# Drawn orders of weight tiles and drawn places of moving tiles in a two-layer decoder trunk

## The chip, the cores and the metric

The kernel runs on one core of one Trainium2 chip. TensorE (PE) multiplies, VectorE (DVE), ScalarE (ACT) and GpSimd (POOL) do the elementwise work, and the queue of SyncE (SP) starts most DMAs. The metric is the device time of one execution in microseconds; lower is better. All arrays are laid out on the host before the launch, so the order in which weights lie in memory can be chosen freely.

## What is computed

The reference is a trunk of two layers over 256 tokens of width 2048, in float32. Layer 0 mixes tokens with a convolution module, layer 1 with causal stick-breaking attention of 16 heads; each is followed by a gated MLP with a depthwise convolution of width 3. Cut to what matters:

```python
for i in range(DEPTH):
    shift, scale, gate = ada_ln(c, mix_mod_w[i], mix_mod_b[i])
    h = rms_norm(x, mix_norm_g[i]) * (1.0 + scale) + shift
    if i % N_MIXERS == 0:
        y = conformer_conv_module(h, ...)    # h @ pw1, gate, conv of width 31, layer norm, silu, @ pw2
    else:
        y = stick_breaking_mixer(h, ...)     # h @ qkv, attention per head, @ o
    x = x + gate * y
    shift, scale, gate = ada_ln(c, ffn_mod_w[i], ffn_mod_b[i])
    h = rms_norm(x, ffn_norm_g[i]) * (1.0 + scale) + shift
    u = causal_depthwise_conv(h @ up_w[i], ...)
    gt, val = jnp.split(u, 2, axis=-1)
    x = x + gate * ((jax.nn.silu(gt) * val) @ down_w[i])
return rms_norm(x, final_norm_g)
```

Widths: the up product gives 2 x 5632 columns, the down product takes 5632 rows.

## The kernel before

**Tiles.** Activations are held transposed, as 128 features by 256 tokens. A product has an output for each 128 columns of its weight matrix (a block of outputs, `nb`) and sums over tiles of 128 rows (`kt`). A weight tile of 128 x 128 is the stationary operand, an activation tile the moving one. There are 16 tiles of the normed input `h` (and of `z`, the convolution module's second input), 44 of the gated MLP's `g`, worked on in two halves of 22, and 16 of the heads' results `o`.

**Split numbers.** Weights and activations are each split into a rounded part and a rest (`wh`, `wl`; `xh`, `xl`), held in a 4-byte type that TensorE multiplies in one pass. A unit of work, one weight tile with one activation tile, is wh·xh + wh·xl + wl·xh. In `gemm` (L270) this is done in one of two forms. As a triple it is three matmuls of 256 columns (L303, L304, L305). As a pair, where `both` is given, one matmul of 512 columns runs over xh and xl together, into a bank with room for both (L298), and one of 256 follows (L299). The second convolution product, the up products of layer 0, and the last output block of each down product run as triples; the down products, the later q and k products, the output projection and layer 1's up products run as pairs.

**Where the halves lie.** `halved` (L374) gives the tiles of z, g and o: one SBUF tile of 2 x HP floats, HP = 264, with the first half at 0 and the second at HP. `h_tiles` (L361) lays h out in the same way. So a tile takes 2112 bytes of each partition, and the next tile of a pool starts 2112 bytes further on. The g tiles stand in a ring of 23 (`g{j % NG}`); z and o have 16 tiles each.

**Order.** `plan` (L46) writes down, for each stage, the order of (output, tile). The first few outputs (`first`) are taken together, tile by tile, so that they can start before all inputs are ready, and they end one after the other on their last `stagger` tiles. The outputs behind them come one by one, each over its tiles in the order of their numbers. `Cfg` (L60) makes the plans: `pw1` and `pw2` for the convolution module, `up{i}0a` to `up{i}1b` and `down{i}0`, `down{i}1` for the MLP of layer i, `qk{g}a`, `qk{g}b` and `v{g}` for groups of four heads, and `o`.

**Streams.** Eight weight tiles make a piece of 512 KB. `_pack` lays the pieces out in the plan's order on the host, `load_next` (L227) loads them in order on SP's queue into a ring of six, `split_next` (L236) splits a piece on ScalarE (L243) and VectorE (L247), and `gemm` takes them piece by piece. When the last tile of an output is done, `done` moves the result on: `pw2_done`, `up_done` (which makes a g tile, L1011 to L1013), `down_done`, `qk_done`, `o_done`. Heads run beside the products, piece by piece (`attention`), and leave their results in o tiles (L1142 to L1145). Modulation vectors are computed on VectorE from streamed matrices (L337), paced by the pieces.

**Stages in time**, from the order of the matmuls, in us from the span's start: first convolution product and convolution to 285, `pw2` to 407, up and down products of layer 0 to 1152, q, k, v and attention to 1452, output projection to 1544, up and down products of layer 1 to 2286, end of the kernel at 2299.

Of the kernel before, what the change touches and what calls it, by code (L numbers as in the profile page):

```python
# [2 lines left out]

# [8 lines left out]
F32R = mybir.dt.float32r  # L12
# [4 lines left out]
P = 128  # L17
# [4 lines left out]
FIRST = 4  # L22
STAGGER = 2
# [19 lines left out]
MORE_MODS = 2  # L43


def plan(nbs, kts, first, stagger=4):  # L46

    seq = []
    if first > 1:
        head, nbs = nbs[:first], nbs[first:]  # L50
        s = min(stagger, len(kts) // 2)
        seq += [(n, k) for k in kts[:len(kts) - s] for n in head]
        seq += [(n, k) for n in head for k in kts[len(kts) - s:]]
    return seq + [(n, k) for n in nbs for k in kts]


class Cfg:
    def __init__(self, D, T, H, F, CW, FW):
        self.D, self.T, self.H, self.F, self.CW, self.FW = D, T, H, F, CW, FW
        KD = self.KD = D // P  # L60
        KF = self.KF = F // P
        self.GH = 4
        self.rows0 = min(ROWS, KD // 4)

        def columns(items):
            cols, n = {}, 0
            for name, k in items:
                cols[name] = (n, n + k)
                n += k
            return cols, n  # L70

        items = []
        items += [("mix_g1", KD), ("mix_b1", 3 * KD)]
        for i in range(2):
            items += [(f"ffn_g{i}", KD), (f"ffn_b{i}", 3 * KD)]
        for i in range(2):
            items += [(f"fdw{i}", 2 * KF * FW), (f"fdb{i}", 2 * KF)]
        items += [("fin_g", KD)]
        self.cols, self.ncols = columns(items)
        items = [("c", KD), ("mix_g0", KD), ("mix_b0", 3 * KD), ("pw1_b", 2 * KD), ("cdw", KD * CW), ("cdb", KD), ("ln_g", KD), ("ln_b", KD),  # L80
                 ("pw2_b", KD)]
        self.ccols, self.nccols = columns(items)

        kd = list(range(KD))
        pl = {}
        pairs = [n for j in range(KD) for n in (j, j + KD)]
        pl["pw1"] = plan(pairs, kd, min(HEAD, 2 * KD), 0)
        pl["pw2"] = plan(kd, kd, 8)
        self.halves = [list(range(KF // 2)), list(range(KF // 2, KF))]
        for i in range(2):  # L90
            for h, js in enumerate(self.halves):
                up = [n for j in js for n in (j, j + KF)]
                if h == 0:
                    pl[f"up{i}0a"] = plan(up[:FIRST], kd, FIRST, STAGGER)
                    pl[f"up{i}0b"] = plan(up[FIRST:], kd, 2, STAGGER)
                else:
                    pl[f"up{i}1a"] = plan(up[:2], kd, 1)
                    pl[f"up{i}1b"] = plan(up[2:], kd, 1)
                pl[f"down{i}{h}"] = plan(kd, js, 4)
        GH = self.GH  # L100
        for g in range(H // GH):
            hs = list(range(g * GH, (g + 1) * GH))
            qk = [n for h in hs for n in (h, H + h)]
            pl[f"qk{g}a"] = plan(qk[:FIRST], kd, FIRST if g == 0 else 1, STAGGER)
            pl[f"qk{g}b"] = plan(qk[FIRST:], kd, 1)
            pl[f"v{g}"] = [(2 * H + h, k) for k in kd for h in hs]
        pl["o"] = plan(kd, list(range(H)), 4)
        self.plans = pl
        order = ["pw1", "pw2", "up00a", "up00b", "up01a", "down00", "up01b", "down01"]
        for g in range(H // GH):  # L110
            order += [f"qk{g}a", f"v{g}"] if g == 0 else [f"v{g}", f"qk{g}a"]
            order.append(f"qk{g}b")
        self.order = order + ["o", "up10a", "up10b", "up11a", "down10", "up11b", "down11"]
# [3 lines left out]
def hybrid_trunk(ctx: ExitStack, tc: tile.TileContext, cfg: Cfg, io: dict):  # L117
    nc = tc.nc
    D, T, H = cfg.D, cfg.T, cfg.H
# [23 lines left out]
    def t256(name="t", bufs=6):  # L143
        return tmp.tile([P, T], F32, name=name, bufs=bufs)
# [23 lines left out]
    def pc(name, i0=0, n=None):  # L168
        if name in cfg.ccols:
            t, (a, b) = cpar["t"], cfg.ccols[name]  # L170
        else:
            t, (a, b) = par, cfg.cols[name]
        return t[:, a:b] if n is None else t[:, a + i0:a + i0 + n]
# [61 lines left out]
    def split_next(later=False):  # L235

        blocks, v, n = raws[len(parts)]
        if stream[len(parts)][0] == "pw1":
            parts.append((blocks, v, None))
            return  # L240
        wh = w_pool.tile([P, PW], F32R, name="wh")
        wl = w_pool.tile([P, PW], F32R, name="wl")
        nc.scalar.copy(wh[:, :n], v[:, :n])  # L243
        parts.append((blocks, wh, wl))

        def low():
            nc.vector.tensor_tensor(wl[:, :n], v[:, :n], wh[:, :n].bitcast(F32), op=ALU.subtract)  # L247

        if later:
            return low  # L250
        low()
# [111 lines left out]
    HP = T + 8  # L363
# [7 lines left out]
    def h_pairs():  # L371
        return [pairs[k] for k in range(KD)]

    def halved(pool, name):  # L374

        v = pool.tile([P, 2 * HP], F32R, name=name).rearrange("p (a t) -> p a t", a=2)[:, :, :T]
        return v[:, 0], v[:, 1], v

    def split_act(t, hh, hl, bias=None):

        if bias is None:
            nc.scalar.copy(hh, t)
            nc.vector.tensor_tensor(hl, t, hh.bitcast(F32), op=ALU.subtract)
        else:
            nc.scalar.activation(hh, t, AF.Identity, bias=bias)
            nc.vector.scalar_tensor_tensor(hl, t, bias, hh.bitcast(F32), op0=ALU.add, op1=ALU.subtract)
# [113 lines left out]
    with ExitStack() as cv:  # L500
# [141 lines left out]
        gb = cpool.tile([P, KD], F32, name="gb")  # L642
# [200 lines left out]
        for c in range(KD + 1):  # L843
# [6 lines left out]
            if c > 0:  # L850
                old = [(c - 1, k) for k in vector_taps(c - 1)[split(c - 1):]]
                n = max(len(taps), len(old))
# [3 lines left out]
            for s in range(nd):  # L856
# [10 lines left out]
                if c == 0 and s % 2 == 1 and 2 + s // 2 < NH:  # L867
                    j = 2 + s // 2
# [5 lines left out]
                if c == KD and s == 0:  # L874
                    low = split_next(later=True)
# [66 lines left out]
        zpool = cpar["z"] = cv.enter_context(tc.tile_pool(name="z", bufs=1))  # L942
        zs, zt = [], []
        for j in range(KD + 1):
            if j < KD:
                zt.append(t256())
                if j > 1:
                    nc.vector.tensor_tensor(ys[j], ys[j], dm, op=ALU.subtract)
                nc.vector.tensor_tensor(zt[j], ys[j], rs, op=ALU.mult)
                nc.scalar.activation(zt[j], zt[j], AF.Silu, bias=pc("ln_b", j, 1), scale=pc("ln_g", j, 1))  # L950
            if j == 1:
                low()
            if j > 0:
                zs.append(halved(zpool, f"z{j - 1}"))
                split_act(zt[j - 1], *zs[j - 1][:2])
            if j in (1, 2, 4):
                split_next()
# [18 lines left out]
    def ffn(i, entry, out):  # L976
        m = f"ffn{i}"
        NG = KF // 2 + 1
        LAST = (KD - 1,)
        with ExitStack() as fs:  # L980
            gpool = fs.enter_context(tc.tile_pool(name=f"g{i}", bufs=1))
            if i == 0:
                more["pool"] = fs.enter_context(tc.tile_pool(name="mods", bufs=MORE_MODS))
            gh, gl, gb = [None] * KF, [None] * KF, [None] * KF
# [17 lines left out]
            def up_done(nb, ps, both=False):  # L1002
                pend[nb] = conv3(ps, nb, both)
                j = nb % KF
                if not (j in pend and j + KF in pend):
                    return
                yg, yv = pend.pop(j), pend.pop(j + KF)
                s = t256()
                nc.scalar.activation(s, yg, AF.Silu)
                nc.vector.tensor_tensor(s, s, yv, op=ALU.mult)  # L1010
                gh[j], gl[j], gb[j] = halved(gpool, f"g{j % NG}")  # L1011
                nc.scalar.copy(gh[j], s)
                nc.vector.tensor_tensor(gl[j], s, gh[j].bitcast(F32), op=ALU.subtract)  # L1013

            def down_done(h):
# [15 lines left out]
                return done  # L1031

            hh, hl = entry.product(f"up{i}0a", up_done, "silu_and_others")
            both = h_pairs() if i else None
            rest = (lambda nb, ps: up_done(nb, ps, True)) if i else up_done
# [48 lines left out]
    with ExitStack() as at:  # L1084
        apool = at.enter_context(tc.tile_pool(name="attn", bufs=1))
# [3 lines left out]
        oh, ol, ob = [None] * H, [None] * H, [None] * H  # L1089
        CO = T + P  # L1090
        qk, vs = {}, {}
# [5 lines left out]
        def attention(h):  # L1097
            q, k, v, vc = qk[h], qk[H + h], vs[h // GH], (h % GH) * P
# [4 lines left out]
            z = zp[:, :CO]  # L1103
# [27 lines left out]
            a = t2.tile([P, CO], F32, name="e", bufs=3)  # L1131
# [7 lines left out]
            nc.tensor.matmul(op[:, 0:P], v[:, 0, vc:vc + P], a[:, 0:P], start=True, stop=True)  # L1139
            nc.tensor.matmul(op[:, P:T], v[:, 0, vc:vc + P], a[:, P:T], start=True, stop=False)  # L1140
            nc.tensor.matmul(op[:, P:T], v[:, 1, vc:vc + P], a[:, T:CO], start=False, stop=True)
            oh[h], ol[h], ob[h] = halved(apool, f"o{h}")  # L1142
            with tc.high_priority(offset=PRIORITY):
                nc.scalar.copy(oh[h], op[:, :T])
                nc.vector.tensor_tensor(ol[h], op[:, :T], oh[h].bitcast(F32), op=ALU.subtract)  # L1145
# [77 lines left out]
    for h in range(2):  # L1223
        t = slice(h * HT, (h + 1) * HT)
        nc.vector.reciprocal(rs[:, t], std[:, t])
        v = mpool.tile([P, D], F32, name="mraw")[:, :KD * HT].rearrange("p (k t) -> p k t", k=KD)
# [129 lines left out]
```

## Time and profile before

| What | Value |
|---|---|
| Median of 3 runs | 2299.14 us (2298.94 to 2299.4) |
| The profiled execution | 2300.79 us, its span 2299.1 us |
| VectorE, ScalarE, GpSimd busy | 1791.5, 1219.0, 409.9 us |
| Matmul and weight-load instructions | 14466 each |
| DMA | 603.16 MB, mean 262 GB/s |
| `up01b`, layer 0, 672 triples | 790.78 to 1025.98 us |
| `up11b`, layer 1, 672 pairs | 1927.78 to 2162.98 us |
| `down10`, layer 1, 330 pairs and 22 triples | 1804.52 to 1927.78 us |

The span runs from the first to the last instruction; the time of the execution is 1.7 us longer. A busy engine in the profile is one with an instruction under way. Matmuls overlap one another in the pipeline, so the mean duration of a matmul in a group is longer than the time from its start to the next one's start; how fast TensorE goes is read from the starts.

### The profile page before, as it was taken

The numbers are of one execution on the slowest core, as the hardware profiler recorded it, in microseconds if no ns is written. First come the engines' busy times: TensorE is split into PE (matmuls) and PEld (weight loads), VectorE is DVE, ScalarE is ACT, GpSimd is POOL, SyncE is SP. The second block draws the span as 40 slices with busy tenths as digits, with TensorE's granted clock in tenths as the row PEclk, the third lists the DMA queues.
The fourth block names the chain that finished last, engine by engine and source line by source line (L and its number), as shares of the span: only waits on it lengthen the run. The fifth ranks groups of instructions, "written<-read, shape, count | busy, mean of one in ns | idle before, by whom it ended". The sixth has DMA issues, their size and how long they took to land.

```text
span 2299.1 us, 37839 instructions
## 1 busy us (share of the span) xinstructions
PE 2265.5 (99%) x14466; PEld 2018.9 (88%) x14466; DVE 1791.5 (78%) x2504; ACT 1219.0 (53%) x1930; POOL 409.9 (18%) x534
## 2 busy tenths in 40 slices
PE   7999999999999999999999999999999999999997
PEld 5888678999998999998898888888888888888887
DVE  7689968989998899999975555779899655777654
ACT  2056655755544455554465555657555544555553
POOL 4058713200003100003411100112000010000031
PEclk9999999999999999999999999999999999999999
DMA  9988798789899989888865555566777665656663
GB/s 396 417 335 303 274 364 349 277 302 338 332 347 338 333 331 341 334 335 303 279 184 161 165 174 172 168 188 234 240 282 275 194 191 185 191 184 189 189 190 110
DMA packets 139144, 603.16 MB, mean 262 GB/s; under 512 B 15441, under 2 KB 15569, under 8 KB 115153
## 3 DMA queue, kind: packets, MB, share of 16 engines
q1 hardware_dynamic: 120242, 464.42, 57.8%
q0 software_dynamic: 18720, 136.32, 16.0%
q8 instruction: 113, 1.85, 0.3%
q14 instruction: 69, 0.57, 0.1%
HBM read 598.58 MB, written 2.10 MB: 261 GB/s over the span
## 4 chain that ended last, share of the span: by engine, by line
PE 86%; DVE 7%; DMA 4%; ACT 1%; issue 1%; POOL 0%; DVEq 0%; SPq 0%; ACTq 0%; POOLq 0%
PE ps L298 32%; PE ps L299 16%; PE ps L303 9%; PE ps L304 9%; PE ps L305 8%; PE ps L689 5%; DMA mraw<-in_mt_mix 3%; DVE mraw L337 3%; DVE wl L247 2%; PE ps L1181 1%; PE ps L1180 1%; PE ps L1179 1%; PE ps L581 1%; DMA raw<-in_w_pw 1%; DMA mraw<-in_mt_ffn 1%
## 5 line engine op out<-in xcount | busy, mean ns | idle before, releaser
L247 DVE TENSOR_TENSOR wl<-raw,wh 128x1024 fp32r<-128x1024 f32 x688 | 848.3, 1239 | 305.0 <-ACT wh L243 303.2
L243 ACT CAST wh<-raw 128x1024 fp32r<-128x1024 f32 x688 | 719.1, 1047 | 665.6 <-PE ps L298 290.2
L298 PE MATMUL ps<-h,wh 128*128 128x512 f32 x1760 | 619.0, 394 | 0.0
L299 PE MATMUL ps<-h,wl 128*128 128x256 f32 x1760 | 493.7, 281 | 0.0
L298 PE MATMUL ps<-g,wh 128*128 128x512 f32 x1320 | 462.5, 394 | 0.0
L303 PE MATMUL ps<-h,wh 128*128 128x256 f32 (+1 forms) x1504 | 421.7, 280 | 0.0
L304 PE MATMUL ps<-h,wh 128*128 128x256 f32 (+1 forms) x1504 | 420.5, 280 | 0.0
L305 PE MATMUL ps<-h,wl 128*128 128x256 f32 (+1 forms) x1504 | 419.0, 279 | 0.1
L298 PEld LDWEIGHTS ps<-h,wh 128*128 128x128 f32 x1760 | 330.5, 188 | 74.4
L337 DVE CUSTOM_DVE_ANT_0 mraw<-mraw,csr 128x2048 f32<-128x2048 f32 x152 | 349.9, 2302 | 30.9 <-DMA mraw<-in_mt_mix 28.7
L299 PE MATMUL ps<-g,wl 128*128 128x256 f32 x1320 | 370.7, 281 | 1.8 <-DVE wl L247 1.6
L299 PEld LDWEIGHTS ps<-h,wl 128*128 128x128 f32 x1760 | 332.3, 189 | 0.2
L298 PEld LDWEIGHTS ps<-g,wh 128*128 128x128 f32 x1320 | 247.8, 188 | 56.6
L304 PEld LDWEIGHTS ps<-h,wh 128*128 128x128 f32 x1504 | 284.7, 189 | 0.1
L305 PEld LDWEIGHTS ps<-h,wl 128*128 128x128 f32 x1504 | 282.5, 188 | 0.7 <-DVE wl L247 0.7
L303 PEld LDWEIGHTS ps<-h,wh 128*128 128x128 f32 x1504 | 282.4, 188 | 0.1
L299 PEld LDWEIGHTS ps<-g,wl 128*128 128x128 f32 x1320 | 249.3, 189 | 3.6 <-DVE wl L247 3.6
L689 PE MATMUL ps<-h,raw 128*128 128x256 f32 x832 | 188.8, 382 | 0.0
L689 PEld LDWEIGHTS ps<-h,raw 128*128 128x128 f32 x832 | 157.8, 191 | 28.3 <-issue 6.7
L1020 POOL TENSOR_TENSOR x<-x,t 128x256 f32<-128x256 f32 x56 | 69.3, 1237 | 533.8 <-ACT t L1019 533.7
L998 DVE SCALAR_TENSOR_TENSOR t<-t,par 128x254 f32<-128x254 f32 (+1 forms) x184 | 88.9, 483 | 46.6 <-ACT t L995 43.7
L729 DVE SCALAR_TENSOR_TENSOR auxb<-u,cpar,auxb 128x256 f32<-128x256 f32 x297 | 121.6, 483 | 4.5 <-ACT auxb L713 3.7
(272 smaller groups left out, 2741.6 us busy)
## 6 DMA issues: line engine op xcount, KB each, us to landing
raw<-in_w_down SPq DMA_DIRECT2D x176, 512.0 KB, 4.1
mraw<-in_mt_ffn POOLq DMA_DIRECT2D x64, 1024.0 KB, 6.4
raw<-in_w_pw SPq DMA_DIRECT2D x96, 512.0 KB, 7.9
mraw<-in_mt_mix POOLq DMA_DIRECT2D x48, 1024.0 KB, 7.8
raw<-in_w_up01b SPq DMA_DIRECT2D x84, 512.0 KB, 6.4
raw<-in_w_up11b SPq DMA_DIRECT2D x84, 512.0 KB, 3.6
raw<-in_w_up00b SPq DMA_DIRECT2D x80, 512.0 KB, 6.2
raw<-in_w_up10b SPq DMA_DIRECT2D x80, 512.0 KB, 4.6
```

The costliest lines, as they stand in the source:

```text
L243: nc.scalar.copy(wh[:, :n], v[:, :n])
L247: nc.vector.tensor_tensor(wl[:, :n], v[:, :n], wh[:, :n].bitcast(F32), op=ALU.subtract)
L298: nc.tensor.matmul(o, wh[:, c], both[kt], start=first, stop=False, skip_group_check=True)
L299: nc.tensor.matmul(o[:, :T], wl[:, c], xh[kt], start=False, stop=left[nb] == 0, skip_group_check=True)
L303: nc.tensor.matmul(o, wh[:, c], xh[kt], start=first, stop=False, skip_group_check=halves > 0)
L304: nc.tensor.matmul(o, wh[:, c], xl[kt], start=False, stop=False, skip_group_check=halves > 0)
L305: nc.tensor.matmul(o, wl[:, c], xh[kt], start=False, stop=left[nb] == 0, skip_group_check=halves > 0)
L337: nc.vector.tensor_tensor_reduce(out=v, in0=v, in1=csr, scale=1.0, scalar=0.0, op0=ALU.mult, op1=ALU.add, accum_out=macc[:, nb:nb + 1])
L689: nc.tensor.matmul(banks[j][:, nb // KD * T:(nb // KD + 1) * T], w[:, b * P:(b + 1) * P], hf[kt], start=first, stop=left[j] == 0, skip_gro ...
L729: nc.vector.scalar_tensor_tensor(conv_ps[j], us[j % UBUFS][:, k:k + T], tap(j, k), conv_ps[j], op0=ALU.mult, op1=ALU.add)
L998: nc.vector.scalar_tensor_tensor(y[:, s:], ps[:, :T - s], w(k), y[:, s:], op0=ALU.mult, op1=ALU.add)
L1020: nc.gpsimd.tensor_tensor(xs[nb], xs[nb], t, op=ALU.add)
```

## The change

The plans get a random generator with a fixed seed. Behind the head of a stage, each output takes its tiles in an order drawn for it; the head keeps its order. Stages without `draw` (`pw1`, `up{i}0a`, `qk{g}a`, and `v{g}`, which has no plan of this kind) keep theirs. The host packs the weights by the plans, so the weights come in the drawn order.

Tiles of g (the inputs of the second products of the MLPs) and of o get a first half at a drawn offset of 0 to 56 floats, in steps of 8, and a second half 256 floats plus a drawn gap of 0 to 56, in steps of 8, behind the first. The tile is as long as that needs. Tiles of z, and those of h, stay as they were.

```diff
-def plan(nbs, kts, first, stagger=4):
-
-    seq = []
+def plan(nbs, kts, first, stagger=4, draw=None):
+
+    seq, drawn = [], draw or random.Random(0)
     if first > 1:
         head, nbs = nbs[:first], nbs[first:]
         s = min(stagger, len(kts) // 2)
         seq += [(n, k) for k in kts[:len(kts) - s] for n in head]
         seq += [(n, k) for n in head for k in kts[len(kts) - s:]]
-    return seq + [(n, k) for n in nbs for k in kts]
+    return seq + [(n, k) for n in nbs for k in (drawn.sample(kts, len(kts)) if draw else kts)]
...
-        pl["pw2"] = plan(kd, kd, 8)
+        draw = random.Random(1)
+        pl["pw2"] = plan(kd, kd, 8, draw=draw)
...
                     pl[f"up{i}0a"] = plan(up[:FIRST], kd, FIRST, STAGGER)
-                    pl[f"up{i}0b"] = plan(up[FIRST:], kd, 2, STAGGER)
+                    pl[f"up{i}0b"] = plan(up[FIRST:], kd, 2, STAGGER, draw)
                 else:
-                    pl[f"up{i}1a"] = plan(up[:2], kd, 1)
-                    pl[f"up{i}1b"] = plan(up[2:], kd, 1)
-                pl[f"down{i}{h}"] = plan(kd, js, 4)
+                    pl[f"up{i}1a"] = plan(up[:2], kd, 1, draw=draw)
+                    pl[f"up{i}1b"] = plan(up[2:], kd, 1, draw=draw)
+                pl[f"down{i}{h}"] = plan(kd, js, 4, draw=draw)
...
-            pl[f"qk{g}b"] = plan(qk[FIRST:], kd, 1)
+            pl[f"qk{g}b"] = plan(qk[FIRST:], kd, 1, draw=draw)
...
-        pl["o"] = plan(kd, list(range(H)), 4)
+        pl["o"] = plan(kd, list(range(H)), 4, draw=draw)
...
-    def halved(pool, name):
-
-        v = pool.tile([P, 2 * HP], F32R, name=name).rearrange("p (a t) -> p a t", a=2)[:, :, :T]
+    def halved(pool, kind, name):
+
+        if kind == "z":
+            at, low = 0, HP
+        else:
+            draw = random.Random(kind + name + "1")
+            at, low = 8 * draw.randrange(8), T + 8 * draw.randrange(8)
+        v = pool.tile([P, at + (2 * HP if kind == "z" else low + T)], F32R, name=name)
+        v = bass.AP(tensor=v.tensor, offset=v.offset + at, ap=[list(v.ap[0]), [low, 2], [1, T]])
         return v[:, 0], v[:, 1], v
...
-                zs.append(halved(zpool, f"z{j - 1}"))
+                zs.append(halved(zpool, "z", f"z{j - 1}"))
...
-                gh[j], gl[j], gb[j] = halved(gpool, f"g{j % NG}")
+                gh[j], gl[j], gb[j] = halved(gpool, f"g{i}", f"g{j % NG}")
...
-            oh[h], ol[h], ob[h] = halved(apool, f"o{h}")
+            oh[h], ol[h], ob[h] = halved(apool, "o", f"o{h}")
```

More of the change, by code (lines that the diff above doesn't have):

```diff
@@ L1 @@
 import math
+import random
 from contextlib import ExitStack
```

## The prediction

> **What bounds the kernel now.** The span and the clock come first, then the page's busy line and the chain that ended last.
>
> ```profile
> core 0: 2299.1 us, clock 0.998
> PE 2265.5 (99%) x14466; PEld 2018.9 (88%) x14466; DVE 1791.5 (78%) x2504; ACT 1219.0 (53%) x1930; POOL 409.9 (18%) x534
> PE 86%; DVE 7%; DMA 4%; ACT 1%; issue 1%; POOL 0%; DVEq 0%; SPq 0%; ACTq 0%; POOLq 0%
> PE ps L298 32%; PE ps L299 16%; PE ps L303 9%; PE ps L304 9%; PE ps L305 8%; PE ps L689 5%; DMA mraw<-in_mt_mix 3%; DVE mraw L337 3%; DVE wl L247 2%; PE ps L1181 1%; PE ps L1180 1%; PE ps L1179 1%; PE ps L581 1%; DMA raw<-in_w_pw 1%; DMA mraw<-in_mt_ffn 1%
> ```
>
> TensorE is busy nearly all the time at the full granted clock, and 74% of the chain lies in the five lines of `gemm` (32 + 16 + 9 + 9 + 8). So the question is whether TensorE waits, and if not, how fast it runs. The waits of PE, and the groups of matmuls in two long stages (the second half of the up products in layer 0, and in layer 1), answer this.
>
> ```profile
> PE auxb L689 <- ACT h L665: 10.4, 4, 9.3
> PE ps L299 <- DVE wl L247: 1.6, 3, 0.7
> ACT wh L243 <- PE ps L298: 290.2, 232, 1.8
> 790.78:1025.98 235.20, 235.20 (x2018) 235.20 (x2017) 216.45 (x275) 123.21 (x180) 16.42 (x31) 1.00 0.89 332
> L303 PE MATMUL ps<-h,wh 128*128 128x256 f32 x672 | 187.9, 280 | 0.0
> 1927.78:2162.98 235.20, 235.20 (x1346) 206.45 (x1345) 169.09 (x248) 133.60 (x206) 0.00 (x0) 1.00 0.61 188
> L298 PE MATMUL ps<-h,wh 128*128 128x512 f32 x672 | 235.2, 393 | 0.0
> ```
>
> In the last four rows a window's columns are its length and the busy times of PE, weight loads, DVE, ACT and POOL; a group's are count, busy time, mean and idle time. I call one tile's work for one block of outputs a unit. In layer 0 it is three matmuls of 256 columns (a triple, L303 to L305), in the other stage one of 512 and one of 256 (a pair, L298 and L299). Each of the two stages holds 672 units, and each takes 235.20 us: **350.0 ns per unit**, for triples and pairs alike, with no idle time before their matmuls. Weight splits on ScalarE wait for PE (290.2 us), not the other way round. So in these stages the time is the number of units times the rate at which TensorE gets through them, and only a change of rate can count.
>
> **Does the rate depend on order and place?** In these stages the tiles come in the order of their numbers. A tile is 2 x 264 floats, 2112 bytes, so successive starts move by 64 bytes within 256 and repeat every four tiles. Elsewhere the trace has other orders. I take the start of a unit, and that of a later one, from the order of instructions, and count the units between.
>
> ```profile
> 1920.05 0.29 PE L303 MATMUL ps<-g,wh 128*128 128x256 f32 x1
> 1923.23 0.28 PE L303 MATMUL ps<-g,wh 128*128 128x256 f32 x1
> 1927.43 0.28 PE L303 MATMUL ps<-g,wh 128*128 128x256 f32 x1
> 1927.78 0.39 PE L298 MATMUL ps<-h,wh 128*128 128x512 f32 x1
> 385.10 0.28 PE L303 MATMUL ps<-z,wh 128*128 128x256 f32 x1
> 389.71 0.28 PE L303 MATMUL ps<-z,wh 128*128 128x256 f32 x1
> 311.16 0.28 PE L303 MATMUL ps<-z,wh 128*128 128x256 f32 x1
> 313.30 0.28 PE L303 MATMUL ps<-z,wh 128*128 128x256 f32 x1
> ```
>
> The first four rows are the last block of outputs of a second product, 22 triples that follow pairs. Its first 9 units take 3.18 us (353 ns each), the next 12 take 4.20 us (350.0): after a disturbance triples run slow, then settle. The same shows in the second convolution product: 13 units behind a stall take 4.61 us (355 ns), and 6 units that stay on one tile take 2.14 us (357). Pairs look different:
>
> ```profile
> 1568.60 0.39 PE L298 MATMUL auxb<-h,wh 128*128 128x512 f32 x1
> 1576.95 0.40 PE L298 MATMUL auxb<-h,wh 128*128 128x512 f32 x1
> 675.96 0.40 PE L298 MATMUL ps<-g,wh 128*128 128x512 f32 x1
> 692.82 0.40 PE L298 MATMUL ps<-g,wh 128*128 128x512 f32 x1
> 1843.11 0.40 PE L298 MATMUL ps<-g,wh 128*128 128x512 f32 x1
> 1912.35 0.40 PE L298 MATMUL ps<-g,wh 128*128 128x512 f32 x1
> 1477.15 0.39 PE L298 MATMUL ps<-o,wh 128*128 128x512 f32 x1
> 1482.75 0.39 PE L298 MATMUL ps<-o,wh 128*128 128x512 f32 x1
> ```
>
> Two units per tile (the first 24 of `up10b`): 8.35 us, 348 ns. Four per tile (48 units at the head of `down00`): 16.86 us, 351.25 ns. Nine whole blocks of `down10`, 198 units: 69.24 us, 349.7 ns. Their 22 tiles are no multiple of four, so each block ends with a jump of another size; 7.693 us a block less 20 units at 350 leaves 693 ns for the two around the jump, 346.5 each. A block of 16 in the output projection: 5.60 us, 350.0. So neither the order nor the place is free, but the whole spread is 346 to 357 ns, 3%.
>
> **The change, part by part.** It adds and removes no instruction: as many matmuls, splits, evictions and DMAs, of the same shapes. The weights are packed on the host in the drawn order, so each DMA still reads one contiguous piece of 512 KB. No wait is added: drawn blocks come behind the undrawn head of their stage, when all their input tiles exist, and the tiles of g are overwritten only behind whole products. The wider tiles cost SBUF, not time. What is left is the rate, stage by stage; for each kind I take the row nearest to "another jump at every unit".
>
> - Triples in drawn order: `up00b` 38 outputs of 16 units, `up01a` 2, `up01b` 42, together 1312 units. Drawn jumps should keep them in the unsettled state. I take 354, between the 353 and the 355 of the two unsettled stretches: 1312 x 4.0 = **+5.2 us**. Bounds: 348 as for pairs (-2.6 us) and 357 as on one tile (+9.2 us).
> - Pairs in drawn order on h: `up10b` 608, `up11a` 32, `up11b` 672, `qk0b` to `qk3b` 256, together 1568 units. I take 348, the row with two kinds of jump in turn: 1568 x -2.0 = **-3.1 us**. Bounds: 346.5 (-5.5 us) and 354, the triples' value (+6.3 us).
> - Pairs in drawn order and at drawn places: 11 blocks of 22 units in each of four second products, 968 units, from 349.7 to 348: **-1.6 us** (bounds -3.1 and +4.2). Output projection, 12 x 16 = 192 units, from 350 to 348: **-0.4 us** (-0.7 and +0.8). No row shows a gap other than 8 floats between the halves; I treat it as one more kind of jump.
> - The heads of these products, 4 x 88 + 64 = 416 units, get drawn places but keep their order; I leave them at 351.25: **0** (346.5 would give -2.0 us, 354 +1.1 us).
> - The last block of each second product, 88 triples, now 7.73 us / 22 = 351.4 on average, goes to 354: **+0.2 us** (bounds -0.3 and +0.5).
> - The second convolution product, 8 drawn blocks, already runs at 355 between its stalls: **0**.
> - Evictions into g and o write as many bytes at other offsets, and ACT and DVE have slack behind PE: **0**. If PE sped up in layer 0's up stage, DVE, busy 216.45 of 235.20 us there, still has 8% left.
>
> Sum: 5.2 - 3.1 - 1.6 - 0.4 + 0.2 = **+0.3 us**. The profiled execution took 2300.79 us for a span of 2299.1; the median of the runs shown is 2299.14. The stages summed here are in that span, so I add the difference to the median: **2299.4 us**.
>
> **The rivals.**
>
> *Nothing of it counts.* TensorE's reads are limited to a fixed rate and the deviations above only follow stalls: 2299.1 us. For it: exactly 350.0 in both forms. Against it: the nine blocks at 349.7 and the head at 351.25, which last for tens of microseconds without a stall. The Trainium skill (SBUF — State Buffer, "Who interferes with whom") says as much as this rival: TensorE has two independent read ports and never waits for anyone. The trace does not bear that out to the last per cent, since 348 and 357 stand beside 350.0.
>
> *Pairs come unsettled as triples do (slower).* Mechanism: the 350.0 is a pattern that locks in only with a constant step from tile to tile, and any other order pays until it locks again. Place: the 2728 drawn pairs. Price: 354 for them adds 6.3 + 4.2 + 0.8 us, the heads 1.1, with 5.2 + 0.5 for the triples: +18.1 us, **2317 us**. It needs less to show: if the pairs merely keep their rate, the triples' +5.4 us alone give 2304.5. The forecast's gains on pairs are 5.1 us, so this side begins where pairs stay above about 349.6. For it: triples do just this, and four units per tile cost 351.25. Against it: pairs at 348 with two kinds of jump.
>
> *Pairs gain more and triples stay (faster).* If every drawn jump is like the one at the end of a block of `down10`, pairs go to 346.5: 5.5 + 3.1 + 0.7 = -9.3 us; with triples still at 350, **2289.8 us**. For it: that jump repeats its gain in all nine blocks. Against it: triples lose at the same jump (353 in the first units of their block).
>
> **How the numbers follow.** The forecast's case (triples lose about what pairs win) has 0.38, nothing counts 0.10, pairs unsettled 0.30, pairs gain more 0.22. A measurement of this kernel tells about 0.2%, 4.6 us, from no change. Within it lie the second case and nearly all of the first, less what spills to either side: same 0.45, slower 0.32, faster 0.23. The range 2289 to 2312 reaches the third rival's end and two thirds of the way to the second's; about 2 in 10 stays outside, mostly above.
>
> **What would show it.** In the changed kernel's windows: layer 0's up stage of 672 triples should grow from 235.2 to about 237.9 us, layer 1's of 672 pairs shrink to about 233.9, each second product's 123.3 us lose 0.4. Instruction counts and PE's waits should stay. If the first stage stays at 235.2, the step on triples is wrong; if the second grows, the step on pairs is. A new idle time before PE would refute the claim that only the rate counts.

## The result and the profile after

The changed kernel took 2307.82 us (median of 5 runs, 2306.48 to 2309.72) against 2299.14 for the kernel before in the same session. The ratio is 1.0034, 95% interval 1.0022 to 1.0045: slower by a third of a per cent, inside the range of the prediction, and not the no-change that it forecast. The clock, the page's busy line and its chain (the shares of each engine in the chain of work that ended last), of the changed kernel:

```profile
core 0: 2306.1 us, clock 0.997
PE 2273.1 (99%) x14466; PEld 2024.2 (88%) x14466; DVE 1792.1 (78%) x2504; ACT 1218.8 (53%) x1930; POOL 409.8 (18%) x534
PE 86%; DVE 6%; DMA 5%; ACT 1%; issue 1%; POOL 0%; DVEq 0%; SPq 0%; ACTq 0%; POOLq 0%
```

The counts are those of before, and PE is 7.6 us longer busy in a span that is 7.0 us longer. No wait took the time: the waits of PE that the prediction quoted are there again, with their sizes.

```profile
PE auxb L697 <- ACT h L673: 10.1, 3, 9.3
PE ps L301 <- DVE wl L249: 1.5, 3, 0.7
```

So the same matmuls ran more slowly, and the stages tell which. The windows of the changed kernel (start and end, length, then busy times of PE, weight loads, DVE, ACT, POOL, the granted clock, DMA's share and its rate in GB/s): `up00b`, `up01b`, `up10b`, `up11b`, `down00`, `down11`.

```profile
431.55:659.06 227.51, 227.12 (x1922) 226.91 (x1921) 209.43 (x281) 121.69 (x174) 14.16 (x27) 1.00 0.90 333
793.98:1032.05 238.07, 238.07 (x2019) 238.07 (x2018) 217.06 (x275) 123.04 (x180) 16.40 (x31) 1.00 0.89 328
1574.76:1799.69 224.93, 224.41 (x1282) 196.25 (x1281) 199.47 (x294) 134.12 (x213) 6.88 (x13) 1.00 0.75 264
1934.28:2169.84 235.56, 235.56 (x1347) 206.12 (x1345) 168.98 (x248) 133.68 (x206) 0.00 (x0) 1.00 0.60 187
670.40:793.98 123.58, 123.58 (x728) 108.96 (x727) 104.63 (x105) 53.46 (x61) 27.84 (x33) 1.00 0.92 348
2169.84:2293.25 123.41, 123.41 (x729) 108.84 (x727) 59.51 (x62) 63.49 (x90) 28.44 (x28) 1.00 0.51 155
```

And those of before that were not shown yet: `up00b`, `up10b`, `down00`, `down11`.

```profile
431.53:656.35 224.82, 224.43 (x1923) 224.22 (x1921) 208.91 (x281) 121.92 (x174) 14.16 (x27) 1.00 0.90 337
1568.60:1793.32 224.72, 224.21 (x1282) 196.47 (x1281) 199.58 (x294) 134.02 (x213) 6.87 (x13) 1.00 0.76 265
667.55:790.78 123.23, 123.23 (x728) 108.94 (x727) 104.70 (x105) 53.49 (x61) 28.12 (x33) 1.00 0.93 348
2162.98:2286.21 123.23, 123.23 (x728) 109.04 (x727) 59.60 (x62) 63.49 (x90) 28.42 (x28) 1.00 0.50 155
```

The reader is to see two sizes of loss. Layer 0's up stages, triples, grew by 2.69 us (`up00b`) and 2.87 us (`up01b`); with 0.14 us of `up01a` that is 5.7 of the 7.0 us. `up01b` runs at 238.07 / 672 = 354.3 ns per unit instead of 350.0. Layer 1's up stages, pairs, grew by only 0.2 and 0.36 us (235.56 / 672 = 350.5 ns), the four second products by 0.1 to 0.35 us each.

### The profile page after: what moved, and what is told of

Its sections match the earlier page's. It is cut to its first block, busy times and chain, and to the rows that moved or that the text cites. A ratio compares the mean times of both kernels' runs of the same rounds, so it can differ in the third digit from the quotient of the medians.

```text
span 2306.1 us, 37838 instructions
## 1 busy us (share of the span) xinstructions
PE 2273.1 (99%) x14466; PEld 2024.2 (88%) x14466; DVE 1792.1 (78%) x2504; ACT 1218.8 (53%) x1930; POOL 409.8 (18%) x534
## 4 chain that ended last, share of the span: by engine, by line
PE 86%; DVE 6%; DMA 5%; ACT 1%; issue 1%; POOL 0%; DVEq 0%; SPq 0%; ACTq 0%; POOLq 0%
PE ps L300 32%; PE ps L301 16%; PE ps L305 9%; PE ps L306 9%; PE ps L307 8%; PE ps L697 5%; DMA mraw<-in_mt_mix 3%; DVE mraw L339 3%; DVE wl L249 1%; PE ps L1187 1%; PE ps L1188 1%; PE ps L1189 1%; DMA mraw<-in_mt_ffn 1%; PE ps L589 1%; DMA raw<-in_w_pw 1%
```

## The experiments

Small differences are read from the stages' windows, since the same stage repeats closely from kernel to kernel when nothing in it changes: `up11b` takes 235.19 or 235.20 us again and again below, and `up00b`, which holds a short wait, 224.80 to 224.86. The kernels of the second, third and fourth part below, and the very last one, were executed once each, so their stages are read and not their totals.

### Orders alone, places alone

The first kernel is the changed one with `halved` as before the change:

```diff
-        if kind == "z":
+        if True:
             at, low = 0, HP
...
-        v = pool.tile([P, at + (2 * HP if kind == "z" else low + T)], F32R, name=name)
+        v = pool.tile([P, at + 2 * HP], F32R, name=name)
```

> The drawn orders without the drawn places (all tiles 2 x 264 floats as before). Theory A, the order of the tiles alone costs, and it costs triples: up01b, 672 triples, stays at 238.1 us as in the changed kernel and up00b at 227.5, so 5.7 us of the 7.0 us of span remain or more; total about 2306. Theory B, the places of g and o carry a good part: the second products fall back below 123.3 us and the total to about 2304 or less. The second products tell: 123.58 and 123.37 us (down00, down10) in the changed kernel, 123.23 and 123.26 before.

It took 2306.43 us, ratio to before 1.0028 (1.0018 to 1.0039). Its `up01b` and `down00`:

```profile
793.63:1031.69 238.06, 238.06 (x2019) 238.06 (x2018) 217.06 (x275) 123.09 (x180) 16.45 (x31) 1.00 0.88 328
670.18:793.63 123.45, 123.45 (x728) 109.03 (x727) 104.66 (x105) 53.49 (x61) 28.08 (x33) 1.00 0.93 347
```

The up stage has the whole loss, the second product most of it. The second kernel keeps the drawn places and drops the orders:

```diff
-        draw = random.Random(1)
+        draw = None
```

> The drawn places without the drawn orders. Theory A: only stages that read g and o can move, all up stages at 235.20 us again, total within 1 us of before (2299 to 2300). Theory B: the second products alone cost 1 us or more. If the places help once the order is regular, the second products come out under 123.2 us.

2301.64 us, ratio 1.0002 (0.9993 to 1.0012). Its `up01b` and `down11`:

```profile
790.64:1025.85 235.21, 235.21 (x2019) 235.21 (x2017) 216.46 (x275) 123.20 (x180) 16.43 (x31) 1.00 0.89 332
2163.41:2287.05 123.64, 123.64 (x728) 108.85 (x727) 59.59 (x62) 63.55 (x90) 28.41 (x28) 1.00 0.51 155
```

The up stages are back, and irregular places alone cost a second product up to 0.4 us (123.64 against 123.23), even in regular order. The four second products grew by 0.94 us together, just short of the 1 us that theory B asked for, and the kernel by 0.9 us against before in the same session. So the **orders** carry the loss, and the places add next to nothing once the orders are drawn. Theory A held, narrowly for the second products.

### Is it the irregularity, or the step?

Two kernels keep everything as before the change, but give the up stages other fixed orders:

```diff
+ORDERS = {
+    "up00b": [15, 14, ..., 0],
+    "up01b": [0, 2, ..., 14, 1, 3, ..., 15],
+    "up10b": [15, 14, ..., 0],
+    "up11b": [0, 2, ..., 14, 1, 3, ..., 15],
+}
...
-    return seq + [(n, k) for n in nbs for k in kts]
+    return seq + [(n, k) for n in nbs for k in (order or kts)]
```

> The kernel before, with other fixed orders of the h tiles in the up stages: up00b (608 triples) and up10b (608 pairs) from the last tile to the first (steps of -64 bytes modulo 256), up01b (672 triples) and up11b (672 pairs) first the even tiles, then the odd ones (steps of 128 bytes). Theory A1, a pattern locks in with any constant step: all four stages keep 350.0 ns per unit, up01b and up11b 235.2 us. Theory A2, each jump has a price of its own, and the step of +64 bytes happens to cost 350.0: pairs with steps of 128 bytes come to 347 (from the jumps between the 22 tiles of down01 before), up11b 233.2 us; reversed pairs to about 347, up10b 222.9 us against 224.7; triples differ from 350 in either direction by 1 to 6 ns, 0.6 to 4 us a stage.

`up00b` and `up01b`, then `up10b` and `up11b`:

```profile
430.73:658.57 227.84, 227.47 (x1922) 227.26 (x1921) 209.45 (x281) 121.68 (x174) 14.19 (x27) 1.00 0.89 332
793.02:1031.57 238.55, 238.55 (x2018) 238.55 (x2017) 217.13 (x275) 122.96 (x180) 16.44 (x31) 1.00 0.89 327
1574.16:1799.92 225.76, 225.26 (x1283) 196.68 (x1281) 199.60 (x294) 134.06 (x213) 6.90 (x13) 1.00 0.76 264
1934.38:2169.01 234.63, 234.63 (x1347) 205.46 (x1345) 169.03 (x248) 133.72 (x206) 0.00 (x0) 1.00 0.62 188
```

Regular orders cost triples as much as drawn ones: 235.20 became 238.55 us with steps of 128 bytes (355.0 ns), and reversed, with steps of -64 bytes, 3.02 us more over 608 units, 355.0 too. So A1 fell: a constant step is not enough. Modulo 128 bytes, steps of -64 and +64 are the same, so if places decide, it is not their remainder by 128. Pairs go both ways: +1.04 us reversed (351.7 ns), -0.57 us with steps of 128 bytes (349.2 ns). That is A2's pattern, but its 347 for both was wrong.

The other kernel groups tiles of one residue in `up00b` and `up10b`, and uses one irregular order for all outputs in `up01b` and `up11b`:

```diff
+    "up00b": [0, 4, 8, 12, 1, 5, 9, 13, 2, 6, 10, 14, 3, 7, 11, 15],
+    "up01b": [10, 2, 6, 15, 0, 1, 8, 12, 5, 4, 11, 13, 9, 7, 14, 3],
```

> The kernel before, with up00b and up10b taking tiles of one residue modulo 256 bytes together (0, 4, 8, 12, 1, 5, ...), and up01b and up11b one and the same irregular order for all outputs. Groups: pairs about 351 ns per unit (the heads' row), triples about 357 (the row that stays on one tile), so up00b 229 us against 224.8, up10b 225.3 against 224.7. Fixed irregular order: if a repeated order of 16 could lock in as a whole, 350.0 for both stages (235.2 us); if only equal steps lock in, or each jump has its own price, up01b about 238 us and up11b about 235.6 as with fresh draws.

`up00b` took 227.46 us and `up10b` 225.47 us (354.3 and 351.2 ns over their 608 units; the 357 expected for grouped triples was too high), `up01b` and `up11b`:

```profile
793.17:1031.20 238.03, 238.03 (x2018) 238.03 (x2017) 217.10 (x275) 122.97 (x180) 16.42 (x31) 1.00 0.89 328
1933.78:2169.81 236.03, 236.03 (x1346) 206.30 (x1345) 168.97 (x248) 133.66 (x206) 0.00 (x0) 1.00 0.61 187
```

One irregular order, repeated 42 times, is no better than fresh draws (354.2 and 351.2 ns). Of six orders of triples five lie at 354 to 355, and one, steps of +64 bytes, at 350.0.

### Form or layer?

Triples stand in layer 0, pairs in layer 1. To part the two, layer 1 computes triples; `up10b` keeps its order, `up11b` draws:

```diff
-            both = h_pairs() if i else None
-            rest = (lambda nb, ps: up_done(nb, ps, True)) if i else up_done
+            both, rest = None, up_done
```

> The kernel before with layer 1's up products as triples instead of pairs; up10b keeps the order of the tiles, up11b (672 units) takes fresh drawn orders. Theory F, the form decides (three weight loads per unit against two): up11b as drawn triples takes 354.3 ns per unit, 238.1 us, as up01b does in layer 0, and up10b 350.0 per unit. Theory L, the layer decides (DMA at 0.89 and DVE at 92% in layer 0's up stage, 0.61 and 72% in layer 1's): up11b stays near 350.5 ns, 235.6 us.

```profile
1569.83:1794.63 224.80, 224.42 (x1923) 224.21 (x1921) 186.64 (x256) 121.87 (x174) 6.90 (x13) 1.00 0.76 266
1929.06:2167.26 238.20, 238.20 (x2018) 238.20 (x2017) 154.58 (x207) 120.35 (x165) 0.00 (x0) 1.00 0.59 186
```

Drawn triples take 238.20 us in layer 1 as in layer 0 (354.5 ns), beside a DVE at 65% and DMA at 0.59. Theory F held: the form decides, not the load beside it.

### Places without steps, other weights, another gap

Three kernels move tiles and keep orders where not said otherwise. To make room, each has three row buffers instead of four in the convolution stage; the fewer buffers are not what counts, since `up01b` keeps 235.20 us in the last kernels below, which have three too. In the first, h tiles are 2304 bytes apart, so all start at one place modulo 256 bytes; `up00b` and `up10b` draw. (z also loses the gap between its halves here.)

```diff
-        v = hpool.tile([P, 2 * HP], F32R, name=f"h{i}")
+        v = hpool.tile([P, 2 * HP + 48], F32R, name=f"h{i}")[:, :2 * HP]
```

> The tiles of h are 2304 bytes apart, so that all start at the same place modulo 256 bytes; up00b and up10b in drawn orders, up01b and up11b in the order of numbers. (To make room there is one buffer fewer for rows in the convolution stage, and z has no gap between its halves, so only the up stages are to be compared.) Theory R, only places modulo 256 bytes count: drawn and undrawn stages run at the same time per unit in each layer, whatever it is (351 to 357 for triples, 351 to 358 for pairs, by the rows that stay on one tile). Theory N, something else in the order counts, such as the weights' order in memory or distance between tiles: triples 354 drawn against 350 undrawn, pairs 350.5 against 350.0.

`up00b`, `up01b`, `up10b`, `up11b`:

```profile
431.11:656.55 225.44, 225.21 (x1923) 225.00 (x1921) 208.93 (x281) 121.94 (x174) 14.16 (x27) 1.00 0.90 336
791.02:1026.96 235.94, 235.94 (x2018) 235.94 (x2017) 216.53 (x275) 123.25 (x180) 16.41 (x31) 1.00 0.90 330
1570.08:1798.95 228.87, 228.54 (x1283) 198.87 (x1281) 199.86 (x294) 134.07 (x213) 6.88 (x13) 1.00 0.74 260
1933.59:2166.55 232.96, 232.96 (x1346) 204.63 (x1345) 169.10 (x248) 133.69 (x206) 0.00 (x0) 1.00 0.63 190
```

Triples bear out theory R: drawn, `up00b` is 0.6 us above before, about +1 ns a unit; undrawn, `up01b` at 351.1 ns is +1.1. The drawing itself costs them nothing here. Pairs brought a surprise: 346.7 ns in `up11b` (232.96 / 672), and in `up10b` the slowest seen. Its steady stretch, 512 units between two starts:

```profile
1593.51 0.40 PE L300 MATMUL ps<-h,wh 128*128 128x512 f32 x1
1776.12 0.40 PE L300 MATMUL ps<-h,wh 128*128 128x512 f32 x1
```

182.61 us / 512 = 356.7 ns. That is not the draw either: `up11a`, undrawn and right behind it, took 11.41 us for 32 units, 356.7 as well, and the undrawn head ahead of it had that rate already. Its first 24 units took 8.56 us:

```profile
1570.08 0.40 PE L300 MATMUL auxb<-h,wh 128*128 128x512 f32 x1
1578.64 0.39 PE L300 MATMUL auxb<-h,wh 128*128 128x512 f32 x1
```

With the same places, pairs can run at either of two steady rates.

The second kernel lengthens the tiles of split weights by 128 bytes, so that they start at two places in turn:

```diff
-        wh = w_pool.tile([P, PW], F32R, name="wh")
-        wl = w_pool.tile([P, PW], F32R, name="wl")
+        wh = w_pool.tile([P, PW + 32], F32R, name="wh")
+        wl = w_pool.tile([P, PW + 32], F32R, name="wl")
```

> The kernel before, all orders kept, with the tiles of split weights 128 bytes longer, so that they start at two places modulo 256 bytes in turn instead of one (and one row buffer fewer in the convolution stage, to make room). Theory W, the time of a unit depends on where the weights lie relative to the activations: up01b leaves 235.20 us, upwards by up to 3 us, and up11b by up to 1 us. Theory M, only the moving tiles' places count: all up stages stay at 350.0 ns per unit, 235.20 us.

`up01b` and `up11b`:

```profile
791.28:1027.18 235.90, 235.90 (x2018) 235.90 (x2017) 216.53 (x275) 122.91 (x180) 16.41 (x31) 1.00 0.90 331
1929.07:2164.26 235.19, 235.19 (x1346) 206.23 (x1345) 169.06 (x248) 133.72 (x206) 0.00 (x0) 1.00 0.62 188
```

The place of the weights counts for triples (351.0 instead of 350.0 ns) and not for pairs. Theory W held for the one, M for the other. The third kernel widens the gap in h from 32 to 64 bytes, which makes the step 128:

```diff
-        v = hpool.tile([P, 2 * HP], F32R, name=f"h{i}")
+        v = hpool.tile([P, 2 * HP + 16], F32R, name=f"h{i}")
...
-        return [v[:, a * HP:a * HP + T + 2] for a in range(2)]
+        return [v[:, a * (HP + 8):a * (HP + 8) + T + 2] for a in range(2)]
```

> The kernel before, all orders kept, with h tiles of 2 x 272 floats: the second half 64 bytes instead of 32 behind the end of the first modulo 256, and steps of 128 bytes from tile to tile (one row buffer fewer in the convolution stage). Theory S, 350.0 belongs to the step of 64 bytes with the gap of 32: triples come to 354 to 355 (up01b 238 us), pairs to 349 to 351. Theory U, 350.0 belongs to regular order as such: both up01b and up11b stay at 235.2 us.

`up01b` took 238.55 us, exactly what the step of 128 bytes with the old gap took; `up11b` 235.20 us, 350.0 ns. Theory S held for triples: their 350.0 belongs to the step of 64 bytes.

### A version that beats both

If pairs at one place can run at 346.7 ns, layer 1 should be laid out so. The heads of before that stayed on one tile hint which place is good: 345 to 347 ns where h starts 128 bytes behind the first tile's place. In the head of `up10b` before, the third tile's two units are the first of these, 0.69 us:

```profile
1569.99 0.39 PE L298 MATMUL auxb<-h,wh 128*128 128x512 f32 x1
1570.68 0.40 PE L298 MATMUL auxb<-h,wh 128*128 128x512 f32 x1
```

Layer 0 keeps steps of 64 bytes for its triples. Layer 0's g lies without gaps in this first try, and only the added lines are shown.

```diff
+        at = 16 * (i % 4) if at_h["one"] is None else at_h["one"]
+        v = hpool.tile([P, 2 * HP + 48], F32R, name=f"h{i}")[:, at:at + 2 * HP]
...
+        hp = T if name[0] == "z" or kind in ('g0',) else HP
+        more = 48 if kind in ('g1', 'o') else 0
+        v = pool.tile([P, 2 * hp + more], F32R, name=name)[:, :2 * hp].rearrange("p (a t) -> p a t", a=2)[:, :, :T]
...
+            if i == 0:
+                at_h["one"] = 32
             act_tables("sqrt_and_others")
             gemm(f"down{i}1", gh, gl, down_done(1), quiet=QUIET, both=gb, apart=LAST)
```

> Orders as before the change. Layer 0's up products keep h tiles in steps of 64 bytes (triples at 350.0 ns). From the mixer of layer 1 on, the tiles of h all start at one place modulo 256 bytes, 128 bytes further than in the run with one residue; so do o and layer 1's g. Layer 0's g tiles lie without a gap between their halves, 2048 bytes apart, also all at one place. One row buffer fewer in the convolution stage makes room. Theory K, pairs at one place settle into one of two rates, 346.7 or 356.7 ns, and this place (heads that stay on it before: 345 to 347) leads to 346.7 in every stage: up11b 232.96 us, up10b about 222.6, down10 and down11 about 122.0, o about 89.3; total about 9 us under before, 2290. Theory H, which of the two rates a stage gets hangs on how it began, not on the place: some stages at 356.7 (up11b 239.7), total within 2295 to 2308. Without a gap (down00, down01) no row says anything: 346 to 357 per unit, 121.8 to 125.5 us.

2292.78 us, ratio to before 0.9966 (0.9953 to 0.9978). `up10b`, `up11b`, `down11`, `down00`:

```profile
1566.98:1789.66 222.68, 222.14 (x1282) 193.76 (x1281) 199.37 (x293) 134.06 (x213) 6.89 (x13) 1.00 0.77 267
1922.93:2155.89 232.96, 232.96 (x1347) 203.46 (x1345) 169.00 (x248) 133.65 (x206) 0.00 (x0) 1.00 0.61 190
2155.89:2278.06 122.17, 122.17 (x728) 107.68 (x727) 59.58 (x63) 63.39 (x90) 28.51 (x28) 1.00 0.51 156
666.91:790.71 123.80, 123.80 (x729) 109.47 (x728) 104.75 (x105) 53.51 (x61) 27.84 (x33) 1.00 0.93 347
```

These stages of layer 1, and `down10` (122.17 us), came out as theory K said. The output projection ran at the rate of theory K too (346.6 ns, below), but took 91.57 us: the 89.3 expected for it was too low, and so was the total of 2290. `up01b` is a test on the side: layer 0's h tiles now lie 2304 bytes apart plus the shift, so modulo 512 bytes they stand elsewhere than before and modulo 256 where they stood, and it took 235.25 us here and 235.20 in the kernels that follow. Without a gap, `down00` lost 0.57 us. The companion kernel used another place for h in layer 1 (`at_h["one"] = 16`), no gap in layer 1's g and in o, and layer 0's g as before:

> As the run with one place for layer 1, with another place for h there (64 bytes earlier), and without a gap for layer 1's g and for o; layer 0's g as before the change. Theory K: this place (heads that stay on it before: 349 to 351) gives one rate for up10b, up11a and up11b alike, about 350. Theory H: up10b and up11b differ by about 10 ns per unit, or fall on 346.7 and 356.7. Without a gap: down10, down11 and o tell what it costs pairs, 346 to 357 per unit.

It took 2301.24 us, ratio 1.0003 (0.9994 to 1.0013). `up10b` 224.75 us, `up11b` 235.19 us: 350.0 ns in both, as K said. `down10` without a gap took 123.79 us, 0.5 us more than before.

The last two kernels drop the gapless g of layer 0, and one of them draws orders for layer 1's up and down products behind their heads:

```diff
-        hp = T if name[0] == "z" or kind in ('g0',) else HP
+        hp = T if name[0] == "z" or kind in () else HP
```

> As the first run with one place for layer 1, but layer 0's g tiles as before the change (with the gap, in steps of 64 bytes). Expected of every theory so far: down00 and down01 back to 123.23 and 126.5 us (from 123.80 and 126.86), the rest as in that run, 0.9 us less in all: about 2292, ratio to before 0.996.

> The same, with drawn orders behind the heads in layer 1's up and down products. Theory R, only places modulo 256 bytes count: pairs whose tiles all lie at one place keep 346.7 ns per unit in drawn order too, up11b 232.96 us, down11 122.18; what the changed kernel lost on pairs (350.5) came from changing places, not from the order as such. Theory N, the order as such costs pairs something: up11b at 233.3 us or more.

The first took **2291.55 us, ratio 0.9961 (0.9947 to 0.9975)**, the lowest ratio here, though its interval overlaps that of the first try. The second was executed once, in 2291.64 us; its `up11b` in drawn order:

```profile
1921.94:2154.90 232.96, 232.96 (x1347) 203.45 (x1346) 168.94 (x248) 133.55 (x206) 0.00 (x0) 1.00 0.63 190
```

232.96 us, to the hundredth what it takes undrawn. At this place the order as such costs nothing; theory R held for pairs. The first kernel had a miss, though: its output projection took 1.36 us more than in the run with gapless g (91.57 us), with o at the same places in both. Two starts, 176 units apart, of the kernel with g as before:

```profile
1475.15 0.39 PE L298 MATMUL ps<-o,wh 128*128 128x512 f32 x1
1537.34 0.39 PE L298 MATMUL ps<-o,wh 128*128 128x512 f32 x1
```

and of the one with gapless g:

```profile
1476.16 0.39 PE L298 MATMUL ps<-o,wh 128*128 128x512 f32 x1
1537.17 0.39 PE L298 MATMUL ps<-o,wh 128*128 128x512 f32 x1
```

62.19 us against 61.01: 353.4 and 346.6 ns. Layer 0's g is not the reason. The drawn kernel has the same g as the first one and the same program up to this stage, and yet it took as long as the run with gapless g. The output projections of the first and of the drawn one:

```profile
1450.06:1542.99 92.93, 92.93 (x535) 81.52 (x534) 68.92 (x86) 55.39 (x77) 19.52 (x20) 1.00 0.60 182
1450.12:1541.70 91.58, 91.58 (x534) 80.08 (x534) 68.91 (x86) 55.23 (x77) 19.57 (x20) 1.00 0.60 184
```

Nor did the first kernel's stage begin badly. The first two rows below are 13 units apart in its head, 4.50 us, 346 ns each; the last three are starts of units in a row:

```profile
1463.84 0.39 PE L298 MATMUL ps<-o,wh 128*128 128x512 f32 x1
1468.34 0.39 PE L298 MATMUL ps<-o,wh 128*128 128x512 f32 x1
1471.10 0.39 PE L298 MATMUL ps<-o,wh 128*128 128x512 f32 x1
1471.51 0.50 PE L298 MATMUL ps<-o,wh 128*128 128x512 f32 x1
1471.97 0.39 PE L298 MATMUL ps<-o,wh 128*128 128x512 f32 x1
```

Between the last three, two units took 0.87 us instead of 0.69. The other two kernels have this short break too, 0.86 and 0.87 us for the same two units. Behind it the first kernel ran at 353.4 ns to the end of the stage, and the others at 346.7. So theory H is not out: a break can change the steady rate at this place too. The place makes 346.7 likely, not sure.

## Why the prediction was right and where it was wrong

Three line numbers in the section on the kernel before are off by a few: `Cfg` stands at L57, `split_next` at L235, `h_tiles` at L366.

*Only the rate counts.* Right: counts and waits of PE are unchanged, and nearly all lost time lies in stages where PE idles no longer than before (0.39 us of `up00b` in both kernels, nothing in `up01b`).

*Triples lose.* Right in direction and size: +5.2 us were forecast at 354 ns, 5.7 us were measured at 354.3. The size was partly luck, since 354 came from 9 units and 13 units behind disturbances. The reason given was half right. They do leave a settled state, but the runs with regular steps show that it is not regularity that settles them. Of all that were tried only the step of +64 bytes gave 350.0, and all tiles at one place 351.1; weights at another place lift the 350.0 by 1 ns.

*Pairs gain.* Wrong, and this step decided the sign. 348 ns was taken from the first 24 units of `up10b`, the row with two kinds of jump in turn, for 2728 units; drawn pairs took 350.5 ns. In place of -3.1, -1.6 and -0.4 us came +0.5 for pairs on h, +0.8 for the second products (their last blocks of triples included), and nothing for the output projection. The drawn order and the four fixed ones tried on pairs lie from 349.2 to 351.7 ns, so the row chosen was a favourable pattern and no mean over jumps; the other row at hand, 351.25 from the heads, was nearer. The second rival had named the consequence: once pairs stay above about 349.6, the triples' loss makes the kernel slower. It came out that way, with triples at its price and pairs near their old rate, not at 354. The prediction's own sign of a wrong step on pairs, a growing up stage in layer 1, showed too. The time still lies in the range because the range reached far towards this rival, and not because of the sum.

*Drawn places.* Left at nothing for the heads and treated as one more jump elsewhere. About right: alone they cost 0.0 to 0.4 us per second product and 0.3 us in the output projection, and beside drawn orders the second products differ by 0.1 us either way.

*Nothing of it counts.* Refuted by the changed kernel itself and by the orders-only run, whose intervals exclude 1. The Trainium skill (SBUF — State Buffer, "Who interferes with whom") has TensorE's two read ports independent and TensorE never waiting. That does not cover what was measured here: moving the weights alone took triples from 350.0 to 351.0 ns. Whether a wait at a port is behind it, no run shows.

*The sum* was +0.3 us; the spans differ by 7.0, and nearly all of what is between the two lies with the pairs. The medians differ by 8.7 because the profiled execution of before, 2300.79 us, is 1.7 us above the median of its runs.

## What to carry to other kernels

When an engine is busy all the time and a change adds no instruction, compare the starts of equal instructions in different stages: here a spread of 3% was both the risk and the room. Before an order or a layout is drawn at random, ask whether the regular one already sits on a good setting; for triples here it did, and random was like the other orders tried. For pairs the layout with all moving tiles at one good place was worth 0.4%, and in the one execution with drawn orders there, their order was free.

## What the runs showed of the hardware

- The rate of these matmuls depends on where their moving tiles start modulo 256 bytes, and no run showed an effect of the order beyond that. With all tiles at one place, drawn and undrawn orders agree to 0.01 us in 233 for pairs, and to 0.1 ns in 351 for triples. The figure of 256 is worked out from three runs: reversed order, the same as before modulo 128, cost triples 5 ns a unit, and a layout that is the same modulo 256 but not modulo 512 cost them nothing.
- The steady rates of pairs whose tiles lie at one place come in steps: 346.7, 350.0, 353.4 and 356.7 ns, about 3.3 ns apart, and the same places can show two of them (346.7 and 356.7 in one kernel, 346.6 and 353.4 for o in two). For o the rate changed in the middle of a stage, behind a break of 0.18 us; nearly the same break left it unchanged in two other kernels. What decides beyond the place was not found.
- Triples, with three weight loads a unit, felt the place of the weights (351.0 ns for 350.0), pairs with two did not (350.0). That weight loads and moving reads get in each other's way would fit this, but no run shows it directly.
- No stage of pairs settled below 346.6 ns. By the formula that the Trainium skill gives for the gap of an isolated matmul (TensorE: Matmul & The Clock Gate, "Back-to-back issue gap") a pair would take 325 ns, an estimate from that page, which itself gives less than the formula for streams of 512 columns. The runs here stay 6.7% above the estimate, and did not show what holds them there.
